# A hybrid decoder step on one core: v ahead of q and k in the attention's input stage, row constants moved, and value pages of the paged attention in another order

## The chip, the cores and the metric

The kernel runs on one core of a Trainium2 chip. The metric is the device time of one execution in microseconds; a lower time is better. Besides that time there is one profiled execution, whose trace records the instructions of each engine: TensorE (PE, its weight loads apart as PEld), VectorE (DVE), ScalarE (ACT), GpSimd (POOL), and the queues from which transfers are issued (SPq, ACTq, POOLq). All times below are microseconds.

## What is computed

One layer of a decoder with 1024 new prompt tokens and 64 sample tokens (8 sequences of 8), all in float32. A norm and one input projection feed three groups: RWKV-7 time mixing, a short convolution, and stick-breaking attention. Their outputs go through an output projection, a squared-ReLU MLP, and a gated per-layer embedding.

```python
h = rmsnorm(x, g_mix); proj = h @ w_in
p_rw, p_cv, p_sb = split(proj)
q, k, v = split(p_sb)                       # 8 heads of 64
q, k = rmsnorm(q, q_gain), rmsnorm(k, k_gain)
# attention, prompt: causal over 1024 tokens; sample: 512 cached tokens by page table + 8 new ones
z = q @ k.T * 64**-0.5 + bias
log_beta, log_keep = log_sigmoid(z), log_sigmoid(-z)   # where k_pos < q_pos
wts = exp(log_beta + (reverse_cumsum(log_keep) - log_keep))
o_sb = wts @ v
x = x + concat(o_rw, o_cv, o_sb) @ w_out
x = x + square(relu(rmsnorm(x, g_mlp) @ w_up)) @ w_down
x = x + sigmoid(rmsnorm(x, g_ple) @ w_ple_gate) * (p @ w_ple_proj)
```

The cached keys and values lie in pages of 128 tokens that a page table maps. The outputs are x for prompt and sample, the new k and v rows, and the new states of the RWKV and convolution groups.

## The kernel before

Float32 products are made of three matmuls on split operands: high part by high part, low by high, high by low (`h_hi`, `h_lo`; `wh`, `wl`). Weights arrive by DMA (`wr`), ACT casts the high part, POOL or DVE subtracts the low part.

A scheduler with a model of the engines orders each engine's instructions ahead of time, from the order of the code and its dependences; on the chip each engine and each queue works through its own list in order. So an instruction that waits holds up all that is behind it on the same engine.

Roughly in time (of the profiled execution):

- 0 to 150: the RWKV projections and what precedes the state recurrence.
- 155 to 447: the attention's input stage, together with the start of the RWKV recurrence. `project` (line 784) makes one of q, k, v (`n` = 0, 1, 2) for one half of the heads (`hf`) and two token tiles: 48 matmuls (L791 to L793) into one of two PSUM banks, a copy to SBUF on ACT (`nat`, L798, five buffers) and, for q and k, a norm: square on ACT, reduction L803 on DVE, root on ACT, reciprocal L805 and product L806 on DVE. `keep` writes what is output: k times its gains by POOL (L816), rows of k and v (L820 to L824), and for v the high and low halves (`spl`, L830 on ACT and L831 on DVE) to memory as `v_s` (L832). `stack` (line 835) transposes q or k on TensorE (L840, four to a stack), takes the high half on ACT (L842) and the low half on DVE (L843), and writes both to `stk_s` (L846). `spl` and the halves of a stack share one tag of four buffers. The loop that calls them stands at L851 to L864: half by half, q, then k, then v, with a stack one or two projections behind.
- In the same stretch `wkv_base` (L267 to L285) inverts small triangular blocks in a chain on DVE: for i = 1 to 31 a product (L281, i x i values) and a reduction (L283) that needs it, at the end a copy L284 and the store `t_s` (L285, SP). `wkv_local` then loads `ar` and `bk` (L483, L486) and `TT`, which is read from `t_s` (L491), all on SP; its first matmuls are L508.
- 447 to 570: convolution projections (L169 to L171) and the first half of the prompt's attention (`attention`, matmuls L907, L908 on the stacked q and k, scans L916), then until 900 output projection and MLP of part A and the second half of the attention (from 575 on).
- 900 to 1100: `decode`, the paged attention of the sample tokens, with MLP matmuls of part A (L1087 to L1089) between its steps. `page_rows` (L1097) gives a function that fetches a page by an indirect DMA on POOL (L1110). In `decode` the new rows are loaded (L1128) and put into `Qb` (L1143), the row constants are made (L1147 to L1191: masks of which row belongs to which sequence and head), keys are transposed (L1203), scores made (L1179), and for each of four pairs of sequences the values are multiplied (L1231): four pages of one sequence (`e` = 0) and its new rows, then four of the other. Pages of v have six buffers (`vpg`).
- 1100 to 1600: the MLP of part B; until 1742 the gated embedding.

Of the kernel before, what the change touches and what calls it, by code (L numbers as in the profile page):

```python
# [21 lines left out]
F32 = mybir.dt.float32  # L22
F32R = mybir.dt.float32r
I32 = mybir.dt.int32
AF = mybir.ActivationFunctionType
ALU = mybir.AluOpType
AX = mybir.AxisListType
# [7 lines left out]
NS = NB * NJ  # L35
# [5 lines left out]
PAGES = 4  # L41
# [7 lines left out]
def hybrid_step(ctx: ExitStack, tc: tile.TileContext, I, O):  # L49
# [123 lines left out]
    w_in = I["w_in"][0]  # L173
    W = Weights(wpool)
# [659 lines left out]
    def stack(hf, n, i0, nat):  # L834

        pt = tr_sb()
        p4 = pt.rearrange("p (r i t) -> p r i t", r=2, i=2)
        for r in range(2):
            for i in range(2):
                PE.transpose(p4[:, r, i, :], nat[:, i, r * 128:r * 128 + 128], ident)  # L840
        hl = [sbp.tile([128, 512], F32R, name=f"st{e}", tag="st", bufs=4) for e in "hl"]
        S.activation(hl[0], pt, AF.Copy, scale=gainT[:, n:n + 1])  # L842
        V.scalar_tensor_tensor(hl[1], pt, gainT[:, n:n + 1], f(hl[0]), op0=ALU.mult, op1=ALU.subtract)  # L843
        for e in range(2):
            for s in range(2):
                (S, SP)[e].dma_start(stk_s[n, 4 * hf + s:4 * hf + 4:2, e, :, i0 * 128:i0 * 128 + 256]  # L846
                                     .rearrange("r d t -> d r t"),
                                     f(hl[e])[64 * s:64 * s + 64].rearrange("p (r t) -> p r t", r=2))


    waiting = []  # L851
    for hf in range(2):
        for n in range(3):
            w = W.load(w_in[:, SB0 + 512 * n + 256 * hf:SB0 + 512 * n + 256 * hf + 256])
            for i0 in range(0, 9, 2):
                nat, last = project(hf, n, w, i0)
                keep(hf, n, i0, nat)
                while waiting and (len(waiting) > 1 or n == 2):
                    with tc.issue_after(last.ins):
                        stack(*waiting.pop(0))  # L860
                    if n < 2:
                        break
                if n < 2 and i0 < 8:
                    waiting.append((hf, n, i0, nat))  # L864
    sbp.release()


# [226 lines left out]
    krows = I["cache_k"][0].rearrange("p s h d -> (p s) (h d)")  # L1094
    vrows = I["cache_v"][0].rearrange("p s h d -> (p s) (h d)")

    def page_rows(pool):  # L1097

        idx = pool.tile([128, 32], I32, name="idx")
        pti = pool.tile([128, 32], I32, name="pti")  # L1100
        src = I["page_table"]
        SP.dma_start(pti, bass.AP(tensor=src.tensor, offset=src.offset, ap=[[0, 128], [1, 32]]))
        io = pool.tile([128, 32], I32, name="io")
        G.iota(io, pattern=[[0, 32]], base=0, channel_multiplier=1)
        V.tensor_scalar(idx, pti, 128, None, op0=ALU.mult)
        V.tensor_add(idx, idx, io)

        def page(pool, name, rows_, b, n, bufs):
            t = pool.tile([128, 512], F32, name=name, bufs=bufs)
            G.indirect_dma_start(out=t, out_offset=None, in_=rows_,  # L1110
                                 in_offset=bass.IndirectOffsetOnAxis(ap=idx[:, b * PAGES + n:b * PAGES + n + 1], axis=0))
            return t

        return page

    def decode():


        db = dp.tile([128, 2], F32, name="db")
        src = I["sb_bias"]  # L1120
        for i in range(8):
            SP.dma_start(db[16 * i:16 * i + 16, 0:1],
                         bass.AP(tensor=src.tensor, offset=src.offset + i // 2 * 2, ap=[[1, 2], [0, 8], [1, 1]]))
        V.tensor_scalar(db[:, 1:2], db[:, 0:1], -1.0, None, op0=ALU.mult)
        nat = []
        for n in range(3):
            t = dp.tile([64, 4, 128], F32, name=f"d{n}")
# [16 lines left out]
                              pt[d, 0:256].rearrange("p (r b e q) -> p r b e q", r=4, e=2, q=8)[:, :, :, e, :])  # L1144


        qi = dp.tile([128, 1], I32, name="qi")  # L1147
        G.iota(qi, pattern=[[0, 1]], base=0, channel_multiplier=1)

        def bits(mask, scale):  # L1150
            i = dp.tile([128, 1], I32, name="qm_i", bufs=2)
            V.tensor_scalar(i, qi, mask, None, op0=ALU.bitwise_and)
            t = dp.tile([128, 1], F32, name=f"bits{mask}")
            V.tensor_copy(t, i)
            if scale != 1.0:
                V.tensor_scalar(t, t, scale, None, op0=ALU.mult)
            return t

        qm, lo, pick, rq = bits(7, 1.0), bits(16, 0.5), bits(24, 0.125), bits(103, 1.0)
        hi = dp.tile([128, 1], F32, name="hi")  # L1160
        V.tensor_add(hi, lo, qm)
        kj = dp.tile([128, 4, 8], F32, name="kj")
        G.iota(kj, pattern=[[32, 4], [1, 8]], base=0, channel_multiplier=0, allow_small_or_imprecise_dtypes=True)

        ej = dp.tile([128, 16], F32, name="ej")
        G.iota(ej, pattern=[[1, 16]], base=0, channel_multiplier=0, allow_small_or_imprecise_dtypes=True)
        before = dp.tile([128, 2, 16], F32, name="before")
        V.tensor_scalar(before[:, 0], ej, lo, None, op0=ALU.is_ge)
        V.tensor_scalar(before[:, 1], ej, hi, None, op0=ALU.is_lt)
        V.tensor_mul(before[:, 0], before[:, 0], before[:, 1])  # L1170
        neg = dp.tile([128, 4, NS], F32, name="neg")
        G.memset(neg, -1.0e30)
        for bp in range(4):
            V.tensor_scalar(neg[:, bp, 16 * bp:16 * bp + 16], before[:, 0], 1.0e30, -1.0e30, op0=ALU.mult, op1=ALU.add)

        def scores(ps, bp, keys):
            for e in range(2):
                for r in range(4):
# [5 lines left out]
            scores(pzn[:, bp * NS:bp * NS + NS], bp, (kT, kT))  # L1184
        V.tensor_add(neg, pzn[:, :4 * NS].rearrange("p (b t) -> p b t", b=4), neg)


        own = dp.tile([128, 4], F32, name="own")
        V.tensor_scalar(own, ej[:, 0:4], pick, None, op0=ALU.is_equal)
        same = dp.tile([128, 32], F32, name="same")  # L1190
        V.tensor_scalar(same, kj.rearrange("p r q -> p (r q)"), rq, None, op0=ALU.is_equal)  # L1191
        o32 = dp.tile([128, 4, NS], F32, name="do32")
        for bp in range(4):
            kts = []
# [28 lines left out]
            S.copy(wT[:NS, 4], pt[:NS, :128])  # L1223

            po = pdc()
            for e in range(2):
                for n in range(PAGES + 1):
                    vp = page(dp, "vpg", vrows, 2 * bp + e, n, 6) if n < PAGES else vd.rearrange("t r c -> t (r c)")
                    k = 128 if n < PAGES else NS
                    for r in range(4):  # L1230
                        PE.matmul(po[32 * r:32 * r + 32, e * 128:e * 128 + 128], wT[:k, n, 32 * r:32 * r + 32],  # L1231
                                  vp[:, r * 128:r * 128 + 128], start=n == 0, stop=n == PAGES)
# [230 lines left out]
    km.release()  # L1463
    pre = tc.alloc_tile_pool(name="pages", bufs=1, side="right", reuse_waits="tile")
    page = page_rows(pre)
    first = [page(pre, "kpg", krows, 0, n, 4) for n in range(PAGES)]
    ap = tc.alloc_tile_pool(name="att_b", bufs=1, side="right", reuse_waits="tile")
    run(attention(ap, 2, 4, banks(3, 4), banks(5, 6), banks(7), AB_))
# [120 lines left out]
```

## Time and profile before

| | |
|---|---|
| time, median of three runs | 1735.58 (1730.76 to 1736.79) |
| profiled execution, its own time | 1743.91 |
| its span, first to last instruction | 1742.0 |
| mean granted TensorE clock | 0.978 of full speed |
| moved by DMA | 197.01 MB |

The stretch that holds the input stage has a few groups of idle time on TensorE; from 280 to 450 us it has none. A row of the timeline has the start, the time from the start of the first to the end of the last instruction, the engine, the line, the operation, what it writes and reads, and in brackets how long the engine stood idle ahead of it and what ended that. Groups by line have a count, the busy time and the mean of one in ns, then idle time. A table by stretches has, for each stretch, the busy time of each engine with the number of instructions, the granted clock, the share of the DMA engines and GB/s.

### The profile page before, as it was taken

What the parts mean: (1) busy time and instruction counts of PE and PEld (TensorE: products, weight loads), DVE (VectorE), ACT (ScalarE), POOL (GpSimd) and SP (SyncE); (2) the same over time, 40 slices, a digit from 0 to 9 for tenths busy, and PEclk for the clock granted to TensorE, in tenths of its full rate; (3) what the DMA queues carried; (4) which work ended last, traced back from release to release, by engine and by line L of the source; (5) the groups of instructions that cost most, each with busy time, mean ns of one, the idle gap of its engine ahead of it and who ended that gap; (6) DMA issues with size and microseconds to landing.
All of it is one profiled execution on the core that took longest, in us unless ns stands there. A gap on an engine that the chain in (4) does not pass through costs nothing.

```text
span 1742.0 us, 30723 instructions
## 1 busy us (share of the span) xinstructions
PE 1663.5 (95%) x11901; PEld 1496.9 (86%) x11901; DVE 1109.6 (64%) x1830; ACT 774.8 (44%) x1537; POOL 693.0 (40%) x746
## 2 busy tenths in 40 slices
PE   6999889999999889999999999998999999998998
PEld 5898888888998667888887767988899999998898
DVE  6266863554576659878754444467888878876432
ACT  6634323323353658566543433464444343443421
POOL 4133121212331654433434652376665555544210
PEclk9999999999999899999999999999999999998999
DMA  5134456434623753443244553421322232321211
GB/s 185 50 115 133 104 156 163 118 88 133 160 75 81 247 174 103 126 125 105 88 142 145 180 175 114 162 67 61 106 89 89 86 94 86 94 94 55 64 52 40
DMA packets 207059, 197.01 MB, mean 113 GB/s; under 512 B 58113, under 2 KB 172449, under 8 KB 206786
## 3 DMA queue, kind: packets, MB, share of 16 engines
q1 hardware_dynamic: 197186, 174.08, 33.5%
q0 software_dynamic: 5120, 16.78, 3.2%
q10 hardware_dynamic: 4608, 4.20, 1.0%
q8 instruction: 93, 1.52, 0.4%
q14 instruction: 52, 0.43, 0.1%
HBM read 158.02 MB, written 36.98 MB: 112 GB/s over the span
## 4 chain that ended last, share of the span: by engine, by line
PE 73%; DVE 12%; DMA 5%; issue 3%; ACT 2%; SPq 2%; POOL 1%; ACTq 0%; DVEq 0%; POOLq 0%
PE b L1087 13%; PE b L1089 13%; PE b L1088 13%; PE b L1416 3%; PE b L1415 3%; PE b L1414 3%; PE b L169 2%; PE b L170 2%; PE b L171 2%; DVE base_Q L281 2%; PE b L791 2%; PE b L792 2%; PE b L793 2%; PE b L936 1%; DMA wr<-in_w_out 1%
## 5 line engine op out<-in xcount | busy, mean ns | idle before, releaser
L1068 POOL TENSOR_TENSOR wl<-wr,wh 128x512 fp32r<-128x512 f32 x172 | 236.0, 1381 | 269.1 <-ACT wh L1067 260.2
L1067 ACT CAST wh<-wr 128x512 fp32r<-128x512 f32 x292 | 179.1, 621 | 305.2 <-PE b L1088 205.9
L1087 PE MATMUL b<-ah,wh 128*128 128x288 f32 (+1 forms) x768 | 258.9, 337 | 10.9 <-DVE x L1452 7.9
L1452 DVE TENSOR_TENSOR x<-b,x 128x288 f32<-128x288 f32 (+1 forms) x384 | 199.0, 528 | 98.4 <-PE b L1089 94.0
L1089 PE MATMUL b<-ah,wl 128*128 128x288 f32 (+1 forms) x768 | 254.8, 332 | 0.0
L1088 PE MATMUL b<-al,wh 128*128 128x288 f32 (+1 forms) x768 | 254.1, 331 | 0.0
L1087 PEld LDWEIGHTS b<-ah,wh 128*128 128x128 f32 x768 | 146.7, 191 | 25.7 <-DVE x L1452 12.5
L1087 PE MATMUL b<-nh,wh 128*128 128x512 f32 (+1 forms) x448 | 165.2, 370 | 0.1
L1088 PE MATMUL b<-nl,wh 128*128 128x512 f32 (+1 forms) x448 | 164.9, 368 | 0.3 <-DVE nl L1297 0.3
L1089 PE MATMUL b<-nh,wl 128*128 128x512 f32 (+1 forms) x448 | 164.2, 367 | 0.0
L1089 PEld LDWEIGHTS b<-ah,wl 128*128 128x128 f32 x768 | 146.7, 191 | 11.3 <-issue 0.8
L1088 PEld LDWEIGHTS b<-al,wh 128*128 128x128 f32 x768 | 147.0, 191 | 9.7 <-issue 0.8
L791 PE MATMUL b<-wh,h_hi 128*128 128x256 f32 x432 | 129.2, 299 | 0.0
L159 POOL TENSOR_TENSOR wl<-wr,wh 128x1024 fp32r<-128x1024 f32 x26 | 69.2, 2673 | 149.0 <-ACT wh L158 114.7
L792 PE MATMUL b<-wl,h_hi 128*128 128x256 f32 x432 | 127.0, 294 | 0.0
L793 PE MATMUL b<-wh,h_lo 128*128 128x256 f32 x432 | 125.9, 291 | 0.0
L169 PE MATMUL b<-h_hi,wh 128*128 128x384 f32 (+1 forms) x336 | 115.5, 344 | 1.9 <-ACT xs L330 1.2
L170 PE MATMUL b<-h_lo,wh 128*128 128x384 f32 (+1 forms) x336 | 113.2, 337 | 0.0
L171 PE MATMUL b<-h_hi,wl 128*128 128x384 f32 (+1 forms) x336 | 111.9, 333 | 0.0
L916 DVE TENSOR_TENSOR_SCAN keep<-keep,onesq 128x128 f32<-128x128 f32 (+3 forms) x64 | 94.7, 1481 | 20.9 <-POOL keep L914 19.7
L1068 DVE TENSOR_TENSOR wl<-wr,wh 128x512 fp32r<-128x512 f32 x120 | 100.6, 841 | 6.0 <-ACT wh L1067 3.1
L1068 POOL TENSOR_TENSOR wsl<-s,wsh 128x512 fp32r<-128x512 f32 x64 | 88.5, 1405 | 29.3 <-ACT wsh L1067 29.2
(417 smaller groups left out, 4326.3 us busy)
## 6 DMA issues: line engine op xcount, KB each, us to landing
wr<-in_w_up SPq DMA_DIRECT2D x64, 512.0 KB
wr<-in_w_down SPq DMA_DIRECT2D x64, 512.0 KB
wr<-in_w_in SPq DMA_DIRECT2D x26, 512.0 KB
wr<-in_w_out SPq DMA_DIRECT2D x16, 512.0 KB
xt<-in_x_prompt SPq DMA_DIRECT2D x8, 512.0 KB
stk_s<-sth ACTq DMA_DIRECT2D x32, 128.0 KB
stk_s<-stl SPq DMA_DIRECT2D x32, 128.0 KB
v_s<-spl SPq DMA_DIRECT2D x16, 256.0 KB
```

Source lines behind the costliest of these rows:

```text
L169: PE.matmul(ps[:, :n], wh[:, k, c], a, start=(k == 0), stop=False)
L170: PE.matmul(ps[:, :n], wh[:, k, c], b, start=False, stop=False)
L171: PE.matmul(ps[:, :n], wl[:, k, c], a, start=False, stop=(k == nk - 1))
L791: PE.matmul(o, a, w[0][:, k, :], start=(k == 0), stop=False)
L792: PE.matmul(o, a, w[1][:, k, :], start=False, stop=False)
L793: last = PE.matmul(o, b, w[0][:, k, :], start=False, stop=(k == 7))
L1067: S.copy(h3, src)
L1068: (sub or G).tensor_sub(l3, src, f(h3))
L1087: PE.matmul(ps[:, :n], w(0, k, m), a, start=(k == 0), stop=False)
L1088: PE.matmul(ps[:, :n], w(0, k, m), b, start=False, stop=False)
L1089: PE.matmul(ps[:, :n], w(1, k, m), a, start=False, stop=(k == nk - 1))
L1452: V.tensor_add(p.x[:, m, t0:t0 + n], ps[:, :n], p.x[:, m, t0:t0 + n])
```

## The change

Three things change.

1. The loop of the input stage takes v of both halves first, then q and k of the first half, q and k of the second. Stacks stay two projections behind the loop (before, v's projections let them all run), and those left over are made behind the last projection.
2. The row constants are made by a function of their own, `row_constants`, which is called ahead of the second half of the attention; `db`, the bias of each row's head, is made by one DMA of the eight biases to all rows, a mask, a product and a sum, instead of eight small DMAs.
3. Pages of v have four buffers instead of six, and each is issued behind the page that was fetched last before its pair's products (`fetched`).

```diff
-    for hf in range(2):
-        for n in range(3):
-            w = W.load(w_in[:, SB0 + 512 * n + 256 * hf:SB0 + 512 * n + 256 * hf + 256])
-            for i0 in range(0, 9, 2):
-                nat, last = project(hf, n, w, i0)
-                keep(hf, n, i0, nat)
-                while waiting and (len(waiting) > 1 or n == 2):
-                    with tc.issue_after(last.ins):
-                        stack(*waiting.pop(0))
-                    if n < 2:
-                        break
-                if n < 2 and i0 < 8:
-                    waiting.append((hf, n, i0, nat))
+    for n, hf in ((2, 0), (2, 1), (0, 0), (1, 0), (0, 1), (1, 1)):
+        w = W.load(w_in[:, SB0 + 512 * n + 256 * hf:SB0 + 512 * n + 256 * hf + 256])
+        for i0 in range(0, 9, 2):
+            nat, last = project(hf, n, w, i0)
+            keep(hf, n, i0, nat)
+            if len(waiting) > 1:
+                with tc.issue_after(last.ins):
+                    stack(*waiting.pop(0))
+            if n < 2 and i0 < 8:
+                waiting.append((hf, n, i0, nat))
+    for args in waiting:
+        with tc.issue_after(last.ins):
+            stack(*args)
     sbp.release()
...
+            fetched[0] = G.indirect_dma_start(
+                out=t, out_offset=None, in_=rows_,
+                in_offset=bass.IndirectOffsetOnAxis(ap=idx[:, b * PAGES + n:b * PAGES + n + 1], axis=0))
             return t
...
+    def row_constants(pool):
...
+        qm, lo, pick, rq = bits(7, 1.0), bits(16, 0.5), bits(24, 0.125), bits(103, 1.0)
+        pair, head = bits(96, 0.0625), bits(8, 0.125)
...
+        V.tensor_add(head, head, pair)
...
+        biases = pool.tile([128, 2, 8], F32, name="biases")
+        src = I["sb_bias"]
+        SP.dma_start(biases[:, 0], bass.AP(tensor=src.tensor, offset=src.offset, ap=[[0, 128], [1, 8]]))
+        V.tensor_scalar(biases[:, 1], ej[:, 0:8], head, None, op0=ALU.is_equal)
+        V.tensor_mul(biases[:, 0], biases[:, 0], biases[:, 1])
+        V.reduce_sum(db[:, 0:1], biases[:, 0], axis=AX.X)
+        V.tensor_scalar(db[:, 1:2], db[:, 0:1], -1.0, None, op0=ALU.mult)
+        return db, neg, own, same
+
     def decode():
-        db = dp.tile([128, 2], F32, name="db")
-        src = I["sb_bias"]
-        for i in range(8):
-            SP.dma_start(db[16 * i:16 * i + 16, 0:1],
-                         bass.AP(tensor=src.tensor, offset=src.offset + i // 2 * 2, ap=[[1, 2], [0, 8], [1, 1]]))
-        V.tensor_scalar(db[:, 1:2], db[:, 0:1], -1.0, None, op0=ALU.mult)
...
+            behind = fetched[0].ins
             for e in range(2):
                 for n in range(PAGES + 1):
-                    vp = page(dp, "vpg", vrows, 2 * bp + e, n, 6) if n < PAGES else vd.rearrange("t r c -> t (r c)")
+                    if n < PAGES:
+                        with tc.issue_after(behind):
+                            vp = page(dp, "vpg", vrows, 2 * bp + e, n, 4)
+                    else:
+                        vp = vd.rearrange("t r c -> t (r c)")
...
     page = page_rows(pre)
+    db, neg, own, same = row_constants(pre)
     first = [page(pre, "kpg", krows, 0, n, 4) for n in range(PAGES)]
```

The scheduler makes these lists of it. First DVE at the end of the inversion chain, before (`ss` and `sq` are the sums and squares of the norm):

```order
L283 TENSOR_REDUCE base_X<-base_Q 128x30
L843 SCALAR_TENSOR_TENSOR stl<-b_3689,gainT,sth 128x512
L805 RECIPROCAL ss<-ss 128x8
L281 TENSOR_TENSOR base_Q<-base_Z,base_X 128x961
L803 TENSOR_REDUCE ss<-sq 128x4
L806 TENSOR_TENSOR nat<-nat,ss 128x512
L283 TENSOR_REDUCE base_X<-base_Q 128x31
L805 RECIPROCAL ss<-ss 128x4
L284 COPY base_X<-base_X 128x1024
```

and with the change:

```order
L831 TENSOR_TENSOR spl<-nat,spl 128x4x64 x2
L281 TENSOR_TENSOR base_Q<-base_Z,base_X 128x900
L283 TENSOR_REDUCE base_X<-base_Q 128x30
L281 TENSOR_TENSOR base_Q<-base_Z,base_X 128x961
L283 TENSOR_REDUCE base_X<-base_Q 128x31
L831 TENSOR_TENSOR spl<-nat,spl 128x4x64 x2
L284 COPY base_X<-base_X 128x1024
L803 TENSOR_REDUCE ss<-sq 128x8
L805 RECIPROCAL ss<-ss 128x8
L806 TENSOR_TENSOR nat<-nat,ss 128x512
```

Ten reductions, nine norm products and six low halves of stacks, which stood between the steps of the chain, now stand behind its end; the sixteen subtractions of v stand ahead of it.

Second SP, around the store of the inverse, before (`new_70` and `new_71` are the sample tokens' rows of k and v):

```order
L285 DMA t_s<-base_X 128x2048
L846 DMA stk_s<-stl 64x2x256 x2
L824 DMA out<-nat 128x2x256
L824 DMA out<-kg 128x2x256
L820 DMA new_70<-kg 64x256
L822 DMA out<-kg 64x256
L832 DMA v_s<-spl 128x4x128
L483 DMA ar<-ar_s 128x3x64 x2
L486 DMA ar<-ar_s 128x2x64 x3
L483 DMA bk<-bk_s 128x2x64 x2
L486 DMA bk<-bk_s 128x2x64 x2
L491 DMA TT<-t_s 32x8x32 x4
```

and with the change:

```order
L832 DMA v_s<-spl 128x4x128 x2
L285 DMA t_s<-base_X 128x2048
L820 DMA new_71<-nat 64x256
L822 DMA out<-nat 64x256
L156 DMA wr<-in_w_in 128x4x256
L483 DMA ar<-ar_s 128x3x64 x2
L486 DMA ar<-ar_s 128x2x64 x3
L483 DMA bk<-bk_s 128x2x64 x2
L486 DMA bk<-bk_s 128x2x64 x2
L491 DMA TT<-t_s 32x8x32 x4
```

The loads of `ar` and `bk` stand behind the store in both; fewer stores stand between.

Third TensorE, at the first stack, before (`b_3217` and `b_3288` are banks of projections of q, `b_3275` that of a stack):

```order
L792 MATMUL b_3217<-wl,h_hi_81 128x256
L793 MATMUL b_3217<-wh,h_lo_83 128x256
L840 MATMUL b_3275<-ident,nat 128x128 x4
L791 MATMUL b_3288<-wh,h_hi_80 128x256
L792 MATMUL b_3288<-wl,h_hi_80 128x256
```

and with the change the first matmuls of the recurrence, in the third projection of q (`b_3775`), 551 projection matmuls from the same point on before, 490 now:

```order
L792 MATMUL b_3775<-wl,h_hi_80 128x256
L793 MATMUL b_3775<-wh,h_lo_82 128x256
L508 MATMUL b_1645<-ar,bk 128x128
L508 MATMUL b_1646<-ar,bk 128x128
L508 MATMUL b_1645<-ar,bk 128x128
L508 MATMUL b_1646<-ar,bk 128x128
L791 MATMUL b_3775<-wh,h_hi_80 128x256
```

Before, eight stacks stood ahead of L508, the first of them 96 matmuls after the start of the count; with the change none does, and the first stack stands behind the third projection of q.

More of the change, by code (lines that the diff above doesn't have):

```diff
@@ L1095, in hybrid_step @@
     vrows = I["cache_v"][0].rearrange("p s h d -> (p s) (h d)")
+    fetched = [None]
     def page_rows(pool):
@@ L1109, in page @@
             t = pool.tile([128, 512], F32, name=name, bufs=bufs)
-            G.indirect_dma_start(out=t, out_offset=None, in_=rows_,
-                                 in_offset=bass.IndirectOffsetOnAxis(ap=idx[:, b * PAGES + n:b * PAGES + n + 1], axis=0))
-            return t
-        return page
-    def decode():
-        db = dp.tile([128, 2], F32, name="db")
-        src = I["sb_bias"]
-        for i in range(8):
-            SP.dma_start(db[16 * i:16 * i + 16, 0:1],
-                         bass.AP(tensor=src.tensor, offset=src.offset + i // 2 * 2, ap=[[1, 2], [0, 8], [1, 1]]))
-        V.tensor_scalar(db[:, 1:2], db[:, 0:1], -1.0, None, op0=ALU.mult)
+            fetched[0] = G.indirect_dma_start(
+                out=t, out_offset=None, in_=rows_,
+                in_offset=bass.IndirectOffsetOnAxis(ap=idx[:, b * PAGES + n:b * PAGES + n + 1], axis=0))
@@ new lines, in page, with bits @@
+            return t
+        return page
+    def row_constants(pool):
+        qi = pool.tile([128, 1], I32, name="qi")
+        G.iota(qi, pattern=[[0, 1]], base=0, channel_multiplier=1)
+        def bits(mask, scale):
+            i = pool.tile([128, 1], I32, name="qm_i", bufs=2)
+            V.tensor_scalar(i, qi, mask, None, op0=ALU.bitwise_and)
+            t = pool.tile([128, 1], F32, name=f"bits{mask}")
+            V.tensor_copy(t, i)
+            if scale != 1.0:
+                V.tensor_scalar(t, t, scale, None, op0=ALU.mult)
+            return t
+        qm, lo, pick, rq = bits(7, 1.0), bits(16, 0.5), bits(24, 0.125), bits(103, 1.0)
+        pair, head = bits(96, 0.0625), bits(8, 0.125)
+        hi = pool.tile([128, 1], F32, name="hi")
+        V.tensor_add(hi, lo, qm)
+        V.tensor_add(head, head, pair)
+        kj = pool.tile([128, 4, 8], F32, name="kj")
+        G.iota(kj, pattern=[[32, 4], [1, 8]], base=0, channel_multiplier=0, allow_small_or_imprecise_dtypes=True)
+        ej = pool.tile([128, 16], F32, name="ej")
+        G.iota(ej, pattern=[[1, 16]], base=0, channel_multiplier=0, allow_small_or_imprecise_dtypes=True)
+        before = pool.tile([128, 2, 16], F32, name="before")
+        V.tensor_scalar(before[:, 0], ej, lo, None, op0=ALU.is_ge)
+        V.tensor_scalar(before[:, 1], ej, hi, None, op0=ALU.is_lt)
+        V.tensor_mul(before[:, 0], before[:, 0], before[:, 1])
+        neg = pool.tile([128, 4, NS], F32, name="neg")
+        G.memset(neg, -1.0e30)
+        for bp in range(4):
+            V.tensor_scalar(neg[:, bp, 16 * bp:16 * bp + 16], before[:, 0], 1.0e30, -1.0e30, op0=ALU.mult, op1=ALU.add)
+        own = pool.tile([128, 4], F32, name="own")
+        V.tensor_scalar(own, ej[:, 0:4], pick, None, op0=ALU.is_equal)
+        same = pool.tile([128, 32], F32, name="same")
+        V.tensor_scalar(same, kj.rearrange("p r q -> p (r q)"), rq, None, op0=ALU.is_equal)
+        db = pool.tile([128, 2], F32, name="db")
+        biases = pool.tile([128, 2, 8], F32, name="biases")
[6 more added lines that the diff above has]
+        return db, neg, own, same
@@ L1144, in decode @@
                               pt[d, 0:256].rearrange("p (r b e q) -> p r b e q", r=4, e=2, q=8)[:, :, :, e, :])
[L1147 to L1174, printed above, removed]
         def scores(ps, bp, keys):
@@ L1185, in decode @@
         V.tensor_add(neg, pzn[:, :4 * NS].rearrange("p (b t) -> p b t", b=4), neg)
[L1188 to L1191, printed above, removed]
         o32 = dp.tile([128, 4, NS], F32, name="do32")
```

## The prediction

> **What bounds the kernel now.** I read the page first (busy time of each engine), then TensorE's waits, then the stretch from 160 to 260 us engine by engine.
>
> ```profile
> span 1742.0 us, 30723 instructions
> PE 1663.5 (95%) x11901; PEld 1496.9 (86%) x11901; DVE 1109.6 (64%) x1830; ACT 774.8 (44%) x1537; POOL 693.0 (40%) x746
> ```
>
> TensorE is busy for 1663.5 of 1742.0 us, so 78.5 us is all its idle time. The change leaves its large matmuls as they are, so what it can win is some of that idle time, and time in which TensorE runs at a lowered clock. TensorE's waits by line (total, times, longest), its timeline and a table by stretches say how much lies in the parts that the change touches:
>
> ```profile
> PE b L907 <- DMA stk_q<-stk_s: 1.7, 1, 1.7
> PE b L1179 <- DVE Qb L1143: 1.4, 1, 1.4
> ...
> 183.70 0.65 PE L840 MATMUL b<-ident,nat 128*128 128x128 f32 x4 [3.11 <-DVE nat L806]
> 217.99 1.12 PE L840 MATMUL b<-ident,nat 128*128 128x128 f32 x4 [4.84 <-DVE stl L843]
> 242.82 1.11 PE L840 MATMUL b<-ident,nat 128*128 128x128 f32 x4 [4.40 <-DVE stl L843]
> 256.35 0.71 PE L508 MATMUL b<-ar,bk 64*128 64x128 f32 x8
> ...
> 184.00:187.70 3.70, 3.70 (x21) 3.70 (x20) 3.53 (x11) 1.85 (x4) 0.00 (x0) 0.54 0.07 15
> 215.00:222.00 7.00, 4.01 (x19) 4.01 (x20) 6.97 (x9) 2.08 (x4) 1.28 (x1) 0.51 0.42 112
> 242.00:246.00 4.00, 3.18 (x16) 3.18 (x17) 1.59 (x5) 0.69 (x1) 2.12 (x4) 0.57 0.93 316
> ```
>
> The second block is TensorE's timeline: three of the stacks' transposes (L840) wait, 3.11 + 4.84 + 4.40 = 12.35 us. L508 stands without a wait: its loads were there. The third block is the table by stretches (length, busy us of PE, PEld, DVE, ACT, POOL, then granted clock): behind each wait TensorE runs at about half clock for 3 to 4 us. Busy time times what is missing of the clock: 3.70 x 0.46 + 4.01 x 0.49 + 3.18 x 0.43 = 5.0 us. So the three waits cost 17.4 us in all.
>
> Why DVE is late is seen in its groups between 177.6 and 240.6 us (busy us, mean ns), and in its timeline:
>
> ```profile
> L281 DVE TENSOR_TENSOR base_Q<-base_Z,base_X 128x1 f32<-128x1 f32 (+30 forms) x31 | 26.9, 867 | 6.8 <-DMA base_Z<-l_s 6.2
> L283 DVE TENSOR_REDUCE base_X<-base_Q 128x1 f32<-128x1 f32 (+30 forms) x31 | 15.5, 500 | 0.5
> L806 DVE TENSOR_TENSOR nat<-nat,ss 128x512 f32<-128x512 f32 (+1 forms) x9 | 9.9, 1102 | 0.0
> L803 DVE TENSOR_REDUCE ss<-sq 128x8 f32<-128x512 f32 (+1 forms) x10 | 6.2, 624 | 0.0
> L843 DVE SCALAR_TENSOR_TENSOR stl<-b,gainT,sth 128x512 fp32r<-128x512 f32 x6 | 4.5, 745 | 0.0
> L284 DVE COPY base_X<-base_X 128x1024 f32<-128x1024 f32 x1 | 2.0, 2028 | 0.0
> ...
> 177.62 0.16 DVE L281 TENSOR_TENSOR base_Q<-base_Z,base_X 128x1 f32<-128x1 f32 x1 [6.21 <-DMA base_Z<-l_s]
> 177.81 0.15 DVE L283 TENSOR_REDUCE base_X<-base_Q 128x1 f32<-128x1 f32 x1
> 185.22 0.68 DVE L806 TENSOR_TENSOR nat<-nat,ss 128x512 f32<-128x512 f32 x1
> 198.02 2.85 DVE L806 TENSOR_TENSOR nat<-nat,ss 128x512 f32<-128x512 f32 x1
> 200.80 0.41 DVE L803 TENSOR_REDUCE ss<-sq 128x4 f32<-128x256 f32 x1
> 201.13 2.85 DVE L281 TENSOR_TENSOR base_Q<-base_Z,base_X 128x441 f32<-128x441 f32 x1
> 235.00 2.56 DVE L806 TENSOR_TENSOR nat<-nat,ss 128x512 f32<-128x512 f32 x1
> ```
>
> The inversion chain (L281, L283, L284) and the norms and low halves of q and k (L803 to L806, L843) share one engine, and they hold it without a gap.
>
> **Part 1, the loop order: the three waits go.** All of v (both halves) now comes before q and k, and v has no norm and no stack. TensorE's order has no L840 ahead of L508, so the 12.35 us and their 5.0 us of clock go: 17.4 us.
>
> **What is late next: L508.** On SP, the loads of ar and bk for L508 stand behind the store of the inverse (L285), before as after:
>
> ```profile
> 240.72 0.34 SPq L285 DMA_DIRECT2D t_s<-base_X  x1
> 247.15 2.05 SPq L483 DMA_DIRECT2D ar<-ar_s  x2
> 251.85 0.98 SPq L486 DMA_DIRECT2D bk<-bk_s  x2
> ...
> 192.82 0.28 PE L793 MATMUL b<-wh,h_lo 128*128 128x256 f32 x1
> 192.94 0.28 PE L791 MATMUL b<-wh,h_hi 128*128 128x256 f32 x1
> L831 DVE TENSOR_TENSOR spl<-nat,spl x8: 411/425/555, 242.7 to 280.8; 128x256 fp32r<-128x256 f32 x8
> ```
>
> TensorE is at the first stack at 183.70 - 3.11 = 180.59 us. From there to L508 before runs 455 projection matmuls and seven stacks, after 393 matmuls and no stack. At 0.12 us from one start to the next (192.82 to 192.94) TensorE stands at L508 at 180.6 + 47.2 = 227.8 us.
>
> The chain: 26.9 + 15.5 + 2.0 = 44.4 us of its own from 177.6 us. Alternating operations start some 0.03 us after the end before (177.62 + 0.16 to 177.81; 62 of them, 1.9 us), which gives 223.9. Sixteen subtractions of v (L831, 0.43 us) come between, about 0.35 each, since operations that don't depend on each other overlap by 0.07 or so (198.02 + 2.85 and the next at 200.80; 200.80 + 0.41 and 201.13): 5.6 us, so 229.5 us. The 9.9 + 6.2 + 4.5 us of norms and low halves (L806, L803, L843) stand behind the chain. I take 230. From below: 227.5, if the 2.0 us that one L281 lost (201.13: 2.85, where the mean is 0.87) doesn't recur; from above 233.6, if all that L806 lost at 198.02 and 235.00 (2.85 and 2.56 instead of 0.68 at 185.22, 4.1 us together) now falls on the chain.
>
> The Trainium skill (SBUF — State Buffer, "SBUF: two separate sides") speaks against the change here: a VectorE operation with two inputs from SBUF and a GpSimd operation that reads SBUF lock each other out for a whole instruction. The stretched L806 and L281 are of this kind and no reduction is stretched, so the trace agrees; by the rule the weight splits on GpSimd always hit the chain once the norms are gone, and the sum would go by 233.6.
>
> Behind the chain's end SP issues the store (0.34), two stores of v's last rows and a weight load (0.49 each, as half of the 0.98 at 251.85): 1.8 us. Then the nine loads, 247.15 to 252.83: 5.7 us. The last must land: L508 started 3.5 us after its issue and didn't wait, so between 0 and 3.5; I take 2, the middle. L508 starts at 230 + 9.5 = 239.5 (235.0 to 244.6). **The new wait is 239.5 - 227.8 = 11.7 us** (7.2 to 16.8), and one stretch at half clock behind it, 2.0 us like the longest of the three. Gain of the stage: 17.4 - 13.7 = **3.7 us** (from a loss of 1.4 to a gain of 8.2). Behind the waiting L508 on TensorE stand the rest of q's and k's projections; their copies on ACT and norms on DVE come later by as much, and nobody but TensorE itself waits for those. The nine loads are queued behind the store's wait on SP together with the next weights, which are used only after the whole of q's first half.
>
> The Trainium skill (TensorE: Matmul & The Clock Gate, "What's actually happening") has half speed after an idle window of about 3.4 us, and full speed after a busy one. That the cost is one window for each wait agrees with the rows; a wait of 3.11 us here already had it. By this rule one long wait is cheaper than three short ones by the two stretches saved, which is what the sum has.
>
> **The end of the stage.** The stacks pile up later, and the first attention matmul (L907) now has 48 convolution matmuls ahead of it instead of 120, while its loads are issued behind the last stores. I cost this with the 1.7 us that L907 waited for stk_q before (nothing to 4.8, the longest wait behind a stack): **1.7 us lost**.
>
> **Part 2, row constants.** In the decode some 17 small DVE operations and eight bias DMAs go:
>
> ```profile
> 901.33 0.22 DVE L1152 TENSOR_SCALAR qm_i<-qi 128x1 int32<-128x1 int32 x2 [0.46 <-POOL qi L1148]
> 903.56 0.42 DVE L1174 TENSOR_SCALAR neg<-before 128x16 f32<-128x16 f32 x4
> 897.40 5.33 SPq L1122 DMA_DIRECT2D db<-in_sb_bias  x8
> 902.78 1.78 SPq L1128 DMA_DIRECT2D d<-new  x3
> 917.67 0.32 PE L1179 MATMUL b<-kT,Qb 128*32 128x64 f32 x8 [1.42 <-DVE Qb L1143]
> 575.00:600.00 25.00, 19.71 (x95) 16.68 (x96) 18.24 (x33) 16.64 (x38) 14.77 (x21) 0.76 0.81 256
> ```
>
> The load of the new rows (L1128) stands right behind the 5.33 us of bias DMAs; without them the 1.42 us of waiting for Qb can go: **1.4 us gained**. The same operations with some ten more (3 us on DVE) now run about 575 to 600 us, where DVE is idle for 6.8 us and TensorE for 5.3: hidden there, 0.5 us lost if part is not (nothing to 3).
>
> **Part 3, value pages.** With four buffers and each page issued behind the last fetched one, the four pages of a pair's second half start only when the first half's matmuls are done:
>
> ```profile
> 948.84 0.95 POOL L1110 DMA_INDIRECT vpg<-in_cache_v,idx  x1 [0.30 <-issue]
> PE b L1231 <- issue: 1.3, 4, 0.4
> 950.98 0.68 PE L1231 MATMUL b<-vpg,wT 128*32 128x128 f32 x13 [0.39 <-issue]
> 945.05 1.09 PE L1203 MATMUL b<-ident,kpg 128*128 128x128 f32 x8
> ```
>
> A page costs 1.25 us of POOL (0.95 and 0.30 idle before it), four 5.0 us. TensorE has eight transposes (1.1 us) and 18 to 21 MLP matmuls (0.23 us each) in between, some 5 us. What lies open is the last landing: 0.5 us for each of four pairs, 2.0 us, against 1.3 us of waits at L1231 before: **0.7 us lost** (1.3 gained to 6.7 lost, with 2 us open for each pair). Behind a waiting page on POOL stand pages of k and weight splits, which are due later than the page.
>
> **Sum:** 3.7 - 1.7 + 1.4 - 0.5 - 0.7 = 2.2 us gained on the profiled execution of 1743.9 us (span 1742.0 and 1.9 around it), so 1741.7. The median shown, 1735.6, is 8.3 below that execution; the same 2.2 us makes it **1733.4 us**. About 0.5% (8.7 us) is what a measurement of this kernel tells from no change.
>
> **The rivals.** *L508 hardly waits (28%).* If POOL's splits miss the chain and v's subtractions lie under it, the chain ends at 222.0 to 224, the loads are issued by 229.5 to 231.5 and L508 waits 2 to 5 us. For it: two ar loads took SP 2.05 us while the 1 MB of the store was moving, two bk loads later 0.98, so the nine could be quicker too; against it: the row at 201.13, and the sixteen subtractions have to run somewhere. Gain 17.4 - 3.5 = 14, time 1722.
>
> *The pages decide (15%).* Four buffers serialise fetch and use: if a landing takes some 3 us longer than TensorE's cover, each of four pairs loses it, 12 us, and with the chain at 233.6 nothing is won ahead of it: 1747. It decides from a wait of over 2 us at the second half of a pair. For it: at 945 us POOL was filling six buffers ahead; against it: the scheduler has put MLP matmuls in between.
>
> *The change doesn't do what it says* is contained in the forecast: the waits at L840 go, and the wait at L508 takes their place.
>
> **How the numbers follow.** Forecast 57%, first rival 28%, second 15%. The forecast's own range is 1726 to 1742 (stage +-5, the rest +-3). For 8 in 10 it reaches to most of the first rival and half of the second: 1719 to 1745. Faster by over 0.5%: 0.28; within: 0.57; slower: 0.15.
>
> **What the changed profile would show.** No wait at L840 between 180 and 240 us; one at L508 near 228 us, some 12 us long, with one stretch at half clock behind it; the copy L284 ending near 230; the first L907 waiting for stk_k or stk_q; no wait for Qb; short waits at the second half's pages. The prediction falls if L508 starts before 234 us, or if a wait at the value pages exceeds 2 us.

## The result and the profile after

The changed kernel takes 1744.3 us in the median of seven runs (1738.3 to 1748.3), the kernel before 1736.1 us in seven runs on the same chip (1730.8 to 1738.1): a ratio of 1.0047, with a 95% interval of 1.0027 to 1.0068. It is 8 us slower where 2 us faster was forecast. The page of the changed kernel, its first lines:

```profile
span 1744.7 us, 30704 instructions
PE 1657.0 (95%) x11901; PEld 1492.6 (86%) x11901; DVE 1114.2 (64%) x1840; ACT 775.1 (44%) x1537; POOL 698.0 (40%) x746
```

The work is the same (11901 matmuls); TensorE's idle time is 1744.7 - 1657.0 = 87.7 us, 9.2 more than the 78.5 of before. TensorE's waits by line in the changed kernel (total, times, longest):

```profile
PE b L508 <- DMA bk<-bk_s: 12.5, 1, 12.5
...
PE b L907 <- DMA stk_q<-stk_s: 7.5, 2, 6.3
...
PE b L936 <- DVE beta L918: 3.2, 1, 3.2
...
PE b L840 <- DVE stl L843: 0.7, 1, 0.7
```

The 12.35 us at L840 are down to 0.7, and L508 has 12.5 in their place. What the sum had too small are the 7.5 us at L907 (1.7 before, with 1.7 more in the sum); the 3.2 us at L936 it did not have. Where they lie is best read from three stretches that begin and end at the same matmuls in both kernels: from the first projection (L791) to the first L508 (the head), from there to the end of the recurrence (L681), and from there to the end of its sample part (L600, the tail). Columns are length, busy time of PE, PEld, DVE, ACT, POOL, the clock, DMA share and GB/s. Before:

```profile
155.24:256.35 101.11, 85.13 (x707) 83.02 (x705) 79.66 (x122) 28.96 (x55) 28.47 (x15) 0.93 0.53 143
256.35:438.78 182.43, 180.97 (x2157) 159.31 (x2156) 88.65 (x200) 58.39 (x131) 33.70 (x31) 0.98 0.48 123
438.78:511.63 72.85, 72.28 (x577) 69.21 (x578) 45.98 (x97) 31.04 (x70) 29.01 (x59) 0.98 0.46 124
```

and with the change:

```profile
155.25:241.78 86.53, 70.56 (x615) 68.94 (x613) 68.57 (x102) 21.89 (x42) 20.44 (x9) 0.92 0.61 174
241.78:424.32 182.54, 182.54 (x2181) 161.34 (x2182) 89.52 (x207) 60.67 (x133) 35.59 (x33) 0.98 0.44 110
424.32:517.75 93.43, 83.25 (x640) 79.02 (x641) 51.77 (x103) 34.21 (x75) 32.06 (x56) 0.93 0.41 112
```

Length less busy time is TensorE's idle time. In the head it is 101.11 - 85.13 = 16.0 us before and 86.53 - 70.56 = 16.0 after: one wait for three, as forecast. The clock over the head, 0.93 before and 0.92 after, is no better either. In the tail it was 72.85 - 72.28 = 0.6 us and is 93.43 - 83.25 = 10.2 us. TensorE ends the tail at 517.75 instead of 511.63, 6.1 us late, after having started on the same microsecond.

### The profile page after: what moved, and what is told of

It is laid out like the page before. It is cut to its first block, busy times and chain, and to the rows that moved or that the text cites. A ratio compares the mean times of both kernels' runs of the same rounds, so it can differ in the third digit from the quotient of the medians.

```text
span 1744.7 us, 30704 instructions
## 1 busy us (share of the span) xinstructions
PE 1657.0 (95%) x11901; PEld 1492.6 (86%) x11901; DVE 1114.2 (64%) x1840; ACT 775.1 (44%) x1537; POOL 698.0 (40%) x746
## 4 chain that ended last, share of the span: by engine, by line
PE 80%; DVE 9%; DMA 4%; ACT 3%; issue 2%; POOL 1%; SPq 1%; ACTq 0%; DVEq 0%; POOLq 0%
PE b L1087 13%; PE b L1089 13%; PE b L1088 13%; PE b L1430 3%; PE b L1429 3%; PE b L1428 3%; PE b L793 3%; PE b L791 3%; PE b L169 3%; PE b L792 3%; PE b L170 2%; PE b L171 2%; PE b L936 2%; DVE base_Q L281 1%; PE b L508 1%
## 5 line engine op out<-in xcount | busy, mean ns | idle before, releaser
L1068 POOL TENSOR_TENSOR wl<-wr,wh 128x512 fp32r<-128x512 f32 x172 | 243.5, 1423 | 291.7 <-ACT wh L1067 243.5
L1087 PE MATMUL b<-ah,wh 128*128 128x288 f32 (+1 forms) x768 | 257.4, 335 | 11.6 <-DVE x L1466 9.0
L1089 PEld LDWEIGHTS b<-ah,wl 128*128 128x128 f32 x768 | 145.6, 190 | 10.6
L791 PE MATMUL b<-wh,h_hi 128*128 128x256 f32 x432 | 128.3, 297 | 0.0
L159 POOL TENSOR_TENSOR wl<-wr,wh 128x1024 fp32r<-128x1024 f32 x26 | 69.6, 2691 | 121.2 <-ACT wh L158 92.7
L1087 PEld LDWEIGHTS b<-nh,wh 128*128 128x128 f32 x448 | 84.0, 188 | 21.6 <-DVE x L1389 3.8
```

Of the source, the lines that this page charges most:

```text
L791: PE.matmul(o, a, w[0][:, k, :], start=(k == 0), stop=False)
L1068: (sub or G).tensor_sub(l3, src, f(h3))
L1087: PE.matmul(ps[:, :n], w(0, k, m), a, start=(k == 0), stop=False)
L1089: PE.matmul(ps[:, :n], w(1, k, m), a, start=False, stop=(k == nk - 1))
```

## The experiments

Each kernel was timed in five rounds beside the kernel before on the same chip; ratios are to that, with their 95% intervals. The three idle times (head, middle, tail) are lengths less busy times of the same three stretches in each kernel's profile.

| kernel | ratio | interval | idle: head | middle | tail |
|---|---|---|---|---|---|
| before, against itself | 0.9991 | 0.9973 to 1.0008 | 15.3 | 0.1 | 1.9 |
| the change once more | 1.0057 | 1.0036 to 1.0078 | 14.0 | 0.0 | 10.1 |
| e1_loop | 1.0066 | 1.0041 to 1.0091 | 14.2 | 0.0 | 10.2 |
| e2_rest | 1.0039 | 1.0014 to 1.0065 | 15.5 | 0.0 | 1.0 |
| e2_again | 1.0011 | 0.9989 to 1.0034 | 15.9 | 1.2 | 0.9 |
| e5_stkact | 1.0074 | 1.0048 to 1.0099 | 16.1 | 0.0 | 9.0 |
| e7_stkpool1 | 1.0053 | 1.0035 to 1.0071 | 14.0 | 0.0 | 7.2 |
| e4_aract | 1.0087 | 1.0057 to 1.0116 | 18.0 | 0.0 | 6.4 |
| e4_arpool | 1.0064 | 1.0042 to 1.0086 | 4.9 | 6.6 | 11.2 |
| e8_poolboth1 | 1.0050 | 1.0028 to 1.0072 | 3.5 | 6.8 | 12.3 |
| e3_vlast | 1.0021 | 1.0002 to 1.0040 | 10.8 | 1.4 | 3.5 |
| e11_tail | 1.0097 | 1.0070 to 1.0125 | 13.1 | 1.4 | 8.6 |
| e12_head | 0.9992 | 0.9979 to 1.0005 | 10.6 | 0.8 | 3.5 |
| e13_tail | 1.0060 | 1.0041 to 1.0078 | 12.5 | 1.6 | 8.4 |
| e14_headar | 0.9976 | 0.9958 to 0.9993 | 12.0 | 3.8 | 0.4 |

### Which part of the change: e1_loop, e2_rest, e2_again

e1_loop is the kernel before with the new loop alone, e2_rest the change with the old loop (constants and pages alone).

> Only the loop order of the input stage is changed; row constants and value pages stay as before. Theory A (the loss lies in the input stage: the three waits at L840 are paid back by one at L508, and the attention's first matmul L907 then waits for stacks that now come last): as slow as the whole change, 6 to 9 us over the kernel before, with a wait of some 12 us at L508 and some 7 us at L907. Theory B (the loss lies in the decode, in the four value buffers or the moved constants): within 3 us of the kernel before, or faster.

> Only the row constants and the order and buffers of the value pages are changed; the loop stays as before. Theory A: from 3 us faster to 1 us slower than before, with the three waits at L840 as before and no wait for Qb. Theory B: 6 to 9 us slower than before.

e1_loop is 0.66% slower (some 11 us, more than the 6 to 9 expected) and has the same idle times as the change: the loop makes the loss. Theory B is out as the main cause, but e2_rest was not free either (0.39%), so it was run again.

> Row constants and value pages alone, once more. If the 5 us of the first measurement are theirs: again 3 to 8 us over the kernel before. If they were the scatter of that group: within 3 us of it.

> The kernel before against itself: within 0.25% of itself by every theory; its profile on this chip shows how far the idle time and the time at half clock of one kernel change from execution to execution (idle 76 to 80 us, half clock 22 to 34 us).

The second time e2 is at 1.0011, an interval that holds no change. Between nothing and some 7 us for the constants and pages stays open; one profile of theirs had a span of 1725.6 us, another 1737.1. The kernel before against itself is at 0.9991, so the comparison itself adds nothing; the idle time of its profile, 73.9 us, lies under the 76 to 80 expected.

> The whole change once more, beside the kernels of this group on one chip. From the first measurement (8 us over the kernel before): 5 to 12 us over it, with a wait of 11 to 13 us at L508 and 6 to 10 us at L907.

The change itself repeats: 0.57%, with 10.5 us of waiting at L508 (a little under the 11 to 13 expected) and 6.2 us at L907.

### Is it the queue in front of L907: e5_stkact, e7_stkpool1

SP's row in the changed kernel at the end of the stage shows a plain suspect. The first head's loads (L888) stand behind the stores of the last stacks (L846), though they read data of the first half of the heads that was stored long before:

```profile
449.18 1.24 SPq L846 DMA_DIRECT2D stk_s<-stl  x2
450.46 0.60 SPq L888 DMA_DIRECT2D stk_k<-stk_s  x1
...
452.29 0.79 SPq L888 DMA_DIRECT2D stk_q<-stk_s  x1
```

e5_stkact takes the first head's loads to ACT's queue:

```diff
-                        SP.dma_start(f(o)[64 * e:64 * e + 64], stk_s[n, h, 1 - e, :, r])
+                        (S if q0 == 0 and h < 1 else SP).dma_start(f(o)[64 * e:64 * e + 64], stk_s[n, h, 1 - e, :, r])
```

and so the two lines for stk_k, stk_q and vs.

> The whole change, with the loads of the first head's stacks and values (L886, L888, L891) issued by ACT instead of SP, so that they no longer stand behind the stores of the last stacks on SP. If the wait of 6.25 us at the first L907 is that queue's doing: it goes, with its stretch at half clock, and the time is 6 to 9 us under that of the change, about that of the kernel before. If the data itself is late (the stacks of the first head are stored late, or the space is not free): L907 waits as long as before, and the time stays within 2 us of the change.

The wait for stk_q went, and nothing was won (1.0074). TensorE's timeline of e5_stkact at that place:

```profile
450.71 0.66 PE L840 MATMUL b<-ident,nat 128*128 128x128 f32 x4 [1.02 <-DVE stl L843]
455.93 0.69 PE L907 MATMUL b<-stk_k,stk_q 128*128 128x384 f32 x1 [4.57 <-ACT keep L910]
...
489.14 0.55 PE L936 MATMUL b<-ident,beta 128*128 128x128 f32 x3 [2.42 <-DVE beta L918]
```

L907 started at 444.90 instead of 456.47, 11.6 us sooner, and its third call waits 4.57 us for ACT, whose first operations of the attention stand behind the high half of the last stack and wait for the bias; that load stands on SP behind the same stores. e7_stkpool1 takes bias and loads to POOL's queue (`G.dma_start`).

> The whole change, with the attention's bias and the first head's stacks and values (L873, L888, L886, L891) loaded from POOL's queue. If the pile-up on SP at the end of the input stage makes the wait at L907 (its loads, and the bias that its first ACT operation needs, stand behind the stores of the last stacks): the idle time of TensorE from the end of the recurrence (L681) to the end of its sample part (L600) falls from 10 to under 4 us and the time is 5 to 9 us under that of the change. If the first head's chain of ACT, DVE and TensorE is what is late there: another wait (for keep or beta) takes its place and the time stays within 2 us.

Idle time in the tail is 7.2 us, the ratio 1.0053. L840 now waits 3.5 us for stl, L907 1.4 us for keep, L936 2.3 us for beta. So the queue was the last wait, not the cause. What remains is a chain of short steps on every engine with too little else for TensorE to do; that this is the cause is argued here, and tested below by the order of the projections.

### Is it the queue in front of L508: e4_aract, e4_arpool, e8_poolboth1

```diff
-                        SP.dma_start(t[:, e, j], src[:, j, :, q].rearrange("a p t -> p a t"))
+                        (S if cs == (0, 1) else SP).dma_start(t[:, e, j], src[:, j, :, q].rearrange("a p t -> p a t"))
```

and so the other line of ar and bk; e4_arpool has G in place of S.

> The whole change, with the first ar and bk loads (L483, L486, for chunks 0 and 1) issued by ACT instead of SP, so that they no longer stand behind the store of the inverse. If the wait of 12.45 us at L508 is that queue's doing: it goes or falls under 3 us, and 8 to 14 us are won against the change, unless the inverse itself (TT, still behind the store) is waited for soon after, which would leave 3 to 6 us of the wait. If the loads depend on the inversion chain in another way (its space): L508 waits as long as before.

The wait stayed. The loads' own row (shortest, median and longest issue, first and last start), then SP's and TensorE's timeline of e4_aract:

```profile
L483 ACTq DMA_DIRECT2D ar<-ar_s x2: 366/380/395, 220.7 to 230.6; - x2
```

```profile
227.32 0.91 SPq L832 DMA_DIRECT2D v_s<-spl  x2
228.60 0.33 SPq L285 DMA_DIRECT2D t_s<-base_X  x1
...
239.59 1.31 PE L508 MATMUL b<-ar,bk 64*128 64x128 f32 x8 [14.53 <-issue]
```

On another queue and with ACT free, the first load went at 220.7, but the second only at 230.6, just behind the last store of v (227.32). In the program's list each transfer of SP and ACT waits for the count of one of eight completion semaphores that they share in turn; the second ar load's is that of v's last store, which waits for DVE at the end of the chain. The trace bears it out: ACT's wait ahead of that load ended at 230.59 us, with the landing of a store of L832.

> The whole change, with the first ar and bk loads (chunks 0 and 1) issued from POOL's queue, which has completion semaphores of its own, so that they wait neither in SP's row nor for a store that waits for the chain. If the queue and its semaphores make the wait at L508: no wait at L508 (under 3 us) and TensorE's idle time up to the end of the recurrence falls from 16 to 4 to 8 us, so 8 to 12 us under the change, unless the first stack (L840, now ahead of L508) or TT takes the wait over, which I give 3 to 6 us. If the space of ar hangs on the chain: a wait of over 9 us at L508 or at a memory wait on POOL stays.

> The last two edits together. If both waits are of the queues: idle time of TensorE from 155 us to the end of the sample recurrence falls from 26 to under 14 us, 12 to 20 us under the change and 3 to 10 us under the kernel before. If only one is: as the better of the two alone.

From POOL, whose transfers have other semaphores, the loads were there: L508 doesn't wait, and idle time in the head fell from 14 to 4.9 us. So ar's space does not hang on the chain. But 5 us came back behind L508, where DVE has the first norms ahead of AB (L511), and the tail had 11 to 12 us. e4_arpool:

```profile
250.23 1.11 PE L517 MATMUL b<-ident,bk 128*128 128x128 f32 x4 [5.15 <-DVE AB L511]
...
454.90 0.45 PE L708 MATMUL b<-ident,s_in 64*64 64x64 f32 x2 [5.24 <-DMA s_in<-in_state_wkv]
```

e8_poolboth1, both edits together, waits elsewhere again:

```profile
455.55 0.47 PE L936 MATMUL b<-ident,beta 128*128 128x128 f32 x1 [7.39 <-DVE beta L918]
```

The three idle times add up to 24.1 us in the change on this chip, and to 22.7 and 22.6 in these two. My expectation of 8 to 20 us was a miss: each wait taken out at its own place came up at the next.

### Head or tail: e3_vlast, e11_tail, e12_head, e13_tail

The loop's order has two halves that can be had apart: v's first half in front (head), and k in place of v at the end (tail). e12_head and e13_tail are the kernel before with the loop alone, e3_vlast and e11_tail the same orders with the rest of the change.

```diff
-    for n, hf in ((2, 0), (2, 1), (0, 0), (1, 0), (0, 1), (1, 1)):
+    for n, hf in ((2, 0), (0, 0), (1, 0), (0, 1), (1, 1), (2, 1)):
```

This is e3_vlast and e12_head, where v's last projections also let the stacks run out as before, so that order and this rule are tried together; e11_tail and e13_tail have `((0, 0), (1, 0), (2, 0), (2, 1), (0, 1), (1, 1))`.

> The whole change, but with v's second half projected last (v, q, k, q, k, v), its projections letting the stacks run out as before. If what the change loses is the cover that v's projections gave the last stacks: TensorE's idle time between the end of the recurrence and the end of its sample part falls from 10 to under 3 us, L907 doesn't wait for its loads, and the time is 5 to 10 us under the change, within 4 us of the kernel before. If the loss comes from v standing first (the wait at L508): it stays within 3 us of the change.

> The whole change, but with the first half's q and k first as before and the second half's q and k last as in the change (q, k, v, v, q, k). If the end of the stage is what loses: the three waits at L840 near 180 to 245 us are there (10 to 13 us), L508 doesn't wait, and waits of 6 to 11 us stand at the start of the attention; the time is within 3 us of the change or above it. If v standing first loses: within 3 us of the kernel before.

> The kernel before with the loop order v, q, k, q, k, v alone. If the end of the stage makes the loss: within 4 us of the kernel before (idle time of TensorE up to L508 some 5 us smaller, 2 to 4 us larger behind the recurrence). If the head makes it: 6 us or more over it.

> The kernel before with the loop order q, k, v, v, q, k alone. If the end of the stage makes the loss: 8 to 16 us over the kernel before, with 8 to 11 us of idle time and 3 to 7 us of half clock between the end of the recurrence and the end of its sample part, where the kernel before has 1 to 2 of each. If the head makes it: within 4 us of the kernel before.

The tail alone (e13_tail) costs 0.60%, as much as the whole loop (0.66%) and the whole change; the head alone (e12_head) costs nothing, with an interval of 0.9979 to 1.0005. The stretches of e12_head:

```profile
153.63:242.73 89.10, 78.47 (x645) 76.43 (x643) 74.36 (x111) 24.72 (x47) 22.00 (x11) 0.92 0.54 148
242.73:424.38 181.65, 180.89 (x2198) 160.57 (x2198) 93.68 (x211) 61.28 (x136) 38.21 (x35) 1.00 0.51 130
424.38:505.16 80.78, 77.31 (x597) 73.52 (x597) 49.90 (x97) 31.98 (x72) 29.10 (x59) 0.94 0.40 112
```

and of e13_tail:

```profile
155.39:253.00 97.61, 85.12 (x701) 81.87 (x699) 79.56 (x122) 28.69 (x55) 28.58 (x15) 0.93 0.52 142
253.00:435.66 182.66, 181.10 (x2134) 159.06 (x2134) 80.55 (x191) 54.74 (x121) 30.78 (x28) 0.96 0.46 119
435.66:525.11 89.45, 81.06 (x600) 76.47 (x600) 50.89 (x98) 33.46 (x72) 31.41 (x54) 0.90 0.40 111
```

With v last the tail has 3.5 us of idle time, with k last 8.4, and the clock in it is 0.94 against 0.90. e3_vlast and e11_tail show the same difference with constants and pages added (1.0021 against 1.0097). e3_vlast's 3.5 us in the tail are just over the 3 expected. e11_tail was expected within 3 us of the change or above it, and lies some 7 us above; it keeps what waits at L840 are left (6.9 us), waits 2.3 us at L508, which was not expected, and has the tail as well.

### A version that is faster than both: e14_headar

> e12_head with the first ar and bk loads (chunks 0 and 1) from POOL's queue. If the waits of the head can be won: up to 5 us under e12_head and under the kernel before. If they only move (to the first products behind L508, as in e4_arpool): within 2 us of e12_head.

e14_headar is e12_head with the first ar and bk loads on POOL's queue: 0.9976 of the kernel before, 0.9958 to 0.9993, some 4 us. Its stretches:

```profile
151.40:244.37 92.97, 80.94 (x700) 79.25 (x698) 74.05 (x113) 24.60 (x48) 29.05 (x20) 0.96 0.58 155
244.37:437.22 192.85, 189.10 (x2215) 166.55 (x2214) 93.24 (x212) 63.56 (x141) 38.73 (x35) 0.98 0.47 121
437.22:524.11 86.89, 86.45 (x660) 82.49 (x660) 55.55 (x122) 38.45 (x85) 31.96 (x72) 0.98 0.41 113
```

The head has more idle time than e12_head's (12.0 against 10.6 us) but a clock of 0.96 instead of 0.92, and the tail is back at 0.4 us. So what was won is not the wait at L508, which was 1.0 us in e12_head. Why clock and tail are better is not shown: the list of instructions differs as well (660 matmuls in the tail for 597), and the intervals of e12_head and e14_headar overlap. The same edit was worth nothing on the change itself (e4_arpool), where 6.6 us came back behind L508 and the tail kept its 11.2.

## Why the prediction was wrong, point by point

- **The three waits at L840 go.** Right: the first stack stands at 251.8 us, and no L840 waits before 449 us.
- **The chain ends at 230.** Right within its range: the copy L284 ends at 232.0, and L508 starts late by as much. The upper end's reason was seen as well. DVE's and POOL's timelines with the change:

```profile
195.81 2.08 DVE L831 TENSOR_TENSOR spl<-nat,spl 128x256 fp32r<-128x256 f32 x1
221.09 4.04 DVE L281 TENSOR_TENSOR base_Q<-base_Z,base_X 128x900 f32<-128x900 f32 x1
231.00 1.02 DVE L284 COPY base_X<-base_X 128x1024 f32<-128x1024 f32 x1
...
221.01 6.39 POOL L159 TENSOR_TENSOR wl<-wr,wh 128x1024 fp32r<-128x1024 f32 x2 [23.40 <-ACT wh L158]
```

  L831 took 2.08 us where 0.41 is usual, and one step of the chain 4.04 where its neighbour of 128x841 took 1.76. With the norms gone, the weight splits on POOL (L159) do fall on the chain: both operations ran beside one. The Trainium skill (SBUF — State Buffer, "SBUF: two separate sides") has a VectorE operation with two inputs from SBUF and a GpSimd operation that reads SBUF lock each other out; the trace agrees: 4.04 us beside L159, 1.76 for the slightly smaller neighbour without it.

- **L508 waits 11.7 us from 227.8 us.** Right: it waits 12.45 us and starts at 241.78 (239.5 forecast). SP's row shows the loads behind the store, as worked out:

```profile
232.06 0.33 SPq L285 DMA_DIRECT2D t_s<-base_X  x1
...
235.92 1.05 SPq L483 DMA_DIRECT2D ar<-ar_s  x2
...
239.65 0.92 SPq L486 DMA_DIRECT2D bk<-bk_s  x2
```

- **One stretch at half clock in place of three.** Right in number, too small in size. The changed kernel behind L508, behind L907 and behind L936, and both kernels (changed, then before) behind L442, near the start of the head:

```profile
241.78:248.37 6.59, 6.59 (x34) 5.92 (x35) 2.13 (x4) 0.00 (x0) 0.00 (x0) 0.50 0.49 101
456.40:460.00 3.60, 3.53 (x14) 3.56 (x15) 0.00 (x0) 0.00 (x0) 0.20 (x2) 0.50 0.70 166
483.90:487.50 3.60, 3.55 (x12) 3.55 (x13) 1.12 (x3) 0.75 (x4) 3.47 (x4) 0.53 0.04 13
...
166.44:169.86 3.42, 3.42 (x15) 2.81 (x14) 1.36 (x5) 0.00 (x0) 0.00 (x0) 0.50 0.88 156
...
166.44:169.86 3.42, 3.42 (x28) 3.15 (x27) 1.61 (x5) 0.59 (x1) 0.00 (x0) 1.00 0.87 150
```

  The stretch behind L508 lasts 6.59 us and costs 6.59 x 0.50 = 3.3 us (2.0 forecast). So the term of 3.7 us gained was 17.4 - 12.45 - 3.3 = 1.7 us. In these two profiles not even that shows: L442, which the change doesn't touch, waits 3.51 us and is followed by a stretch at half clock that costs 1.7 us; before, it waits 3.34 us, and the clock stays full. The head then loses 12.45 us of waiting and 5.0 us of clock, where it lost 12.35 and 5.0 before. The two stretches in the tail, 1.8 + 1.7 = 3.4 us, belong to waits that the sum did not have.

- **The end of the stage costs 1.7 us (nothing to 4.8).** This is the step that failed, by its size. The tail's idle time grew by 10.2 - 0.6 = 9.6 us, and the 3.4 us at half clock come on top: 13.0 us where 1.7 were in the sum and 4.8 its upper bound. TensorE's timeline in the tail of the changed kernel:

```profile
449.20 0.65 PE L840 MATMUL b<-ident,nat 128*128 128x128 f32 x4 [0.70 <-DVE stl L843]
456.47 0.76 PE L907 MATMUL b<-stk_k,stk_q 128*128 128x128 f32 x2 [6.25 <-DMA stk_q<-stk_s]
...
483.95 0.47 PE L936 MATMUL b<-ident,beta 128*128 128x128 f32 x1 [3.22 <-DVE beta L918]
```

  I had seen that 48 convolution matmuls instead of 120 stand ahead of L907, and took the price from the wait at that one line. Even that wait stood elsewhere. The kernel before, its last stack, its first L907, and the L907 that waited:

```profile
419.39 0.27 PE L840 MATMUL b<-ident,nat 128*128 128x128 f32 x1
...
467.51 0.22 PE L907 MATMUL b<-stk_k,stk_q 128*128 128x128 f32 x1
...
621.01 0.53 PE L907 MATMUL b<-stk_k,stk_q 128*128 128x512 f32 x2 [1.72 <-DMA stk_q<-stk_s]
```

  The 1.7 us lie at 621 us, in the second half of the attention; the first L907 did not wait at all. What mattered was the work between the last stack and the attention. Before, the last L840 ended at 419.7 us and L907 started at 467.5: 48 us, filled by v's last projections, the last of the recurrence and convolution. With the change they stand at 449.9 and 456.5: 7 us for the low half, the stores, the loads, the bias and the first scores. Nothing on TensorE waits for v's projections before the attention's products with v (L946, first at 478.3 us before), so they cover a chain of other engines well; the change spent them at the head, where they only traded three waits for one. The upper bound of 4.8 us was that of a wait in the middle of the stage, with projections around it, and no bound for a place without them.

  That the change lost some 8 us and not 13 in this pair is partly luck: the profile before lost 1.5 us of waiting and 3.4 us of clock in the middle (L621, see the last section), which neither its second profile nor the changed kernel's shows. The second profiles of both kernels have 10.1 - 1.9 = 8.2 us more idle time in the tail with the change, and 3.0 us more lost to half clock.

- **Qb, 1.4 us gained.** Not borne out. The second profile of the kernel before has no such wait, nor have e1_loop, e12_head and e13_tail, which keep the old decode. I had priced one row of one execution.
- **Constants and value pages, 1.2 us lost together.** Waits at the value pages stayed small, 1.0 us in all at L1245 (2.0 forecast). The constants were not quite hidden: their operations ended two waits at 584 to 587 us, 0.8 and 0.4 us (0.5 forecast). TensorE's waits in the changed kernel:

```profile
PE b L1245 <- issue: 1.0, 1, 1.0
...
PE b L947 <- DVE bits L1131: 0.8, 1, 0.8
```

  The two parts alone measured 1.0039 and 1.0011. Two more pairs differ by them alone: e3_vlast and e12_head (1.0021 and 0.9992), e11_tail and e13_tail (1.0097 and 1.0060). So in four of five comparisons they lose 0.1 to 0.4%; the fifth, the change beside e1_loop (1.0057 and 1.0066), shows none. A loss of a few us is likely, but not shown, since the pairs were timed on different chips.
- **The rivals.** That L508 hardly waits was wrong. A slower outcome was held possible only through the value pages, and it came through the tail of the stage, which the prediction had as a small term of its own. Neither of its two signs of being wrong came (L508 before 234 us, a wait over 2 us at the value pages); it had named none for the tail.

## What to carry to other kernels

Work that nothing waits for (here v's projections) is worth most where a chain of short steps on other engines has nothing else to hide it; before moving it, measure the time between the last producer and the first consumer at the place it leaves, not only the waits at the place it goes to. A wait is a price only for the place where it stands: look up its time before using it elsewhere. When a static order decides, taking out the wait that ended last mostly shows the next one: undo halves of the change, and only then name a queue. A wait of a microsecond in one profile may be absent from the next profile of the same kernel, so it should not be a term of a sum.

## What was not expected of the hardware

Short waits were followed by very different times at half clock. The kernel before waits 1.33 us at L621, and TensorE then runs for 7 us at 0.52 of the clock; e2_again, the same code there, waits 1.07 us and keeps full clock. The kernel before, its timeline and the stretch behind:

```profile
278.48 0.72 PE L621 MATMUL b<-UV,AB 128*64 128x64 f32 x10 [1.33 <-ACT UV L564]
```

```profile
280.00:287.00 7.00, 7.00 (x52) 5.95 (x50) 3.47 (x9) 0.41 (x1) 0.00 (x0) 0.52 0.88 248
```

and e2_again, the same two views:

```profile
278.90 0.72 PE L621 MATMUL b<-UV,AB 128*64 128x64 f32 x10 [1.07 <-ACT UV L564]
```

```profile
280.00:290.00 10.00, 10.00 (x97) 8.59 (x96) 5.98 (x15) 0.66 (x2) 0.00 (x0) 1.00 0.88 247
```

The first lost 7.00 x 0.48 = 3.4 us to it. The length of the wait alone does not decide it: e13_tail waits 0.88 us at L621 and 0.37 us just behind, and runs at 0.50 of the clock from 280.94 to 287.76 us. What does decide is not shown. The two profiles of the kernel before have spans of 1742.0 and 1727.5 us at mean clocks of 0.978 and 0.985; 4.6 us of the difference is idle time. That is why idle times are compared here stretch by stretch, and times only in ratios of many runs.

A second point is of the program more than of the chip: moving a load to another engine's queue did not free it from the first queue (e4_aract), since the completion semaphores are shared in turn.
